# A two-layer transformer trunk on one core: 2048 bytes of descriptor scratch in place of 512, and five small activation buffers in place of six

## The chip, the core and the metric

The kernel runs on one core of a Trainium2 chip. Its engines are TensorE (PE, matrix products), VectorE (DVE), ScalarE (ACT), GpSimd (POOL) and SyncE (SP); each runs its own list of instructions in order, and semaphores hold an instruction back until its inputs are there. Transfers between the off-chip memory (HBM) and the on-chip memory (SBUF, 128 partitions) are issued by SP, ACT or POOL and carried out by 16 DMA engines. The metric is the device time of one execution in microseconds (us). Before the change: median 558.6 of three runs, 558.29 to 560.03.

## What is computed

```python
def reference(x, moba_w_qkv, ..., ln_mlp_b):
    h = x                                     # 1 x 256 x 1024, float32
    for i in range(DEPTH):                    # 2 layers
        if i % 2 == 0:
            mix = moba_attention(h, ...)      # 16 heads of 64
        else:
            mix = dilated_attention(h, ...)   # 12 heads in 3 groups
        h = layer_norm(ALPHA * h + mix, ...)
        h = layer_norm(ALPHA * h + jnp.square(jax.nn.relu(h @ w_in)) @ w_out, ...)
    return h
```

The layers run over 256 tokens of width 1024, and the inner width of the multi-layer perceptron (MLP) is 4096. With 256 tokens and blocks of 256 the block choice of the first layer leaves plain causal attention.

## The kernel before

All weights pass once from HBM through SBUF, and each float32 product is made of three matmuls at reduced input precision: an operand is split into an upper part and a remainder, and upper x upper, upper x lower and lower x upper are added up in PSUM. So each weight tile of 128 x 1024 is loaded by SP into a `raw` buffer (7 of them), ACT writes its upper part to `whi` (L394) and DVE the remainder to `wlo` (L399); `whi` and `wlo` have 10 buffers each. `load_w` (L420) does this. All matmuls stand at L403.

**The second way to load.** `load_far` (L408 to L418) makes the remainder without DVE. ACT copies the upper part (L415) and writes its negative into `wlo` (L416); then POOL issues a transfer from HBM that adds the weight itself onto `wlo` (L417), which leaves weight minus upper part. `FAR` (L41) names the steps that load so: 5 and 14 of the MLP's output projection, in both layers. A step has two tiles, so there are eight such transfers, in four pairs; the tiles meet activations that lie in `sc`. These are the only transfers that POOL issues. The descriptors of a transfer issued by POOL are written into a scratch area of SBUF, whose size, 512 bytes of each partition, is set when the program is made (L1554).

**The MLP.** Its steps are listed in `STEPS`: `f5 f4 f2 f3 O0 f7 f1 O5 f6 ob s2 S8 Oe S4 sa S6 O1 O3 sd O7 o9 z oc Of`. An `f` step multiplies with the first weight matrix, squares and clips. An `o` or `O` step multiplies 256 rows of the second weight matrix. An `s` or `S` step does the same for a two-by-two arrangement of blocks with seven products in place of eight (`do_duo`), from sums of blocks of weights (made by DVE in `raw`) and of activations (`duo_sums`, L637 to L652). `O` and `S` steps have their split activations in the cells of other tensors that are free by then (`sc`, `pt`, `v`, `q0hi` and such); `o` and `s` steps take them from the small activation tiles `ta`.

**The buffers `ta`.** A `ta` tile is 128 x 512 float32, 2048 bytes of each partition. `NTA` (L59) says how many there are. They hold the products of the rotary embedding (L723 and L1102), the squared activations of `O` and `S` steps (`do_first`), the split activations of `o` and `s` steps, and intermediate sums. An `s` step holds five at once: the sums (one) and the two halves each of two splits (four, `spare`, L634). An `o` step holds two. The splits of the step `s2`, the first `s` step, come right behind the step `ob`.

**The order.** The kernel text records operations with a cost each; `Plan.order` (L134 to L304) then simulates the engines and chooses, whenever an engine is free, the operation that can start first (and, of those, the one due first). A buffer is given out when its last user in that simulation is done, so the number of `ta` buffers bears on the order of all engines. The program is then emitted in that order. SBUF is nearly full: the highest address in use ends 256 bytes short of the 229,376 of a partition.

Of the kernel before, what the change touches and what calls it, by code (L numbers as in the profile page):

```python
# [55 lines left out]

OTAGS = {"o": "acc", "p": "tp", "t": "tp"}
HOMES = (("ta", "ta"), ("pt0", "pt1"))
NTA = 6  # L59
NRAW = 7  # L60
NFIRST = 6
PER = 1024 // (NFIRST * P)
# [71 lines left out]
class Plan:  # L134
# [20 lines left out]
    def op(self, eng, cost, fn, reads=(), writes=(), xfer=0.0, early=0.0, ahead=0.0):  # L155
        o = Op()
        o.n, o.eng, o.cost, o.fn, o.xfer = len(self.ops), eng, cost, fn, xfer
        o.early, o.ahead = early, ahead
        o.preds, o.succs, o.bufs = set(), [], set()
        for group, is_write in ((reads, False), (writes, True)):  # L160
            for item in group:
                b, key = item if isinstance(item, tuple) else (item, None)
                o.bufs.add(b)
                for k, st in b.state.items():
                    if key is None or k is None or k == key:
                        if st[0] is not None:
                            o.preds.add(st[0])
                        if is_write:
                            o.preds.update(st[1])
                st = b.state.setdefault(key, [None, []])  # L170
                if is_write:
                    if key is None:
                        b.state = {None: [o, []]}
                    else:
                        st[0], st[1] = o, []
                else:
                    st[1].append(o)
        o.preds.discard(o)
        for p in o.preds:
            p.succs.append(o)  # L180
        for b in o.bufs:
            b.left += 1
            b.ops.append(o)
        self.ops.append(o)
        return o
# [148 lines left out]
def tile_trunk(  # L334
# [37 lines left out]
    def mk(shape, dt, tag, bufs, space=None):  # L372
        uid[0] += 1
        return plan.buf(Bufs(space or sb, bufs), shape, dt, tag, bufs, f"{tag}_{uid[0]}")
# [7 lines left out]
    def act(n, aps=0, sbuf=False):  # L382
        return n / 1200 + (0.093 if sbuf else 0.055) + 0.093 * aps
# [50 lines left out]
    class Stage:  # L434
# [43 lines left out]
        def part(self, j):  # L478
            return next(i for i, (c0, c1) in enumerate(self.parts) if c0 <= S + j * P < c1)
# [154 lines left out]
    def spare():  # L634
        return mk([P, 512], F32R, "ta", NTA), 0, 0

    def duo_sums(u, cells):  # L637

        t, c0, _ = u
        s = mk([P, 512], F32, "ta", NTA)  # L640
        a11, a21, a12, a22 = [part(t, c0 + i * P, P) for i in range(4)]
# [91 lines left out]
    def rotate(xy, ropet):  # L733
# [10 lines left out]
        for half, ps in enumerate(xy):  # L744
            ps = ps()
            b, a = mk([P, 512], F32, "ta", NTA), mk([P, 512], F32, "ta", NTA)
            src = ps
# [122 lines left out]
    def copy_out(n, ps, tag):  # L870
        t = mk([P, 512], F32, tag, NTA if tag == "ta" else 2)
        op("ACT", act(n), lambda: nc.scalar.activation(t.t[:, :n], ps.t[:, :n], AF.Copy), [ps], [t])
        return t
# [238 lines left out]
    def relu_sq_tok(ps, m, ahi, alo):  # L1112
        r = mk([P, 512], F32, "ta", NTA)
        op("ACT", act(512), lambda: nc.scalar.activation(r.t, ps.t, AF.Relu), [ps], [r])
        op("ACT", act(512, 0, True), lambda: nc.scalar.activation(r.t, r.t, AF.Square), [r], [r])
        pt = psum("tp")
        transposes(pt, [(j * P, lambda j=j: r.t[:, j * P : (j + 1) * P]) for j in range(4)], [r], AHEAD["square"])
        t = slice(m * P, (m + 1) * P)
        keys = [(j, m) for j in range(4)]
        split(  # L1120
            512, lambda: pt.t.rearrange("p (j s) -> p j s", j=4), lambda: ahi.t[:, :, t], lambda: alo.t[:, :, t],
            [pt], [(ahi, k) for k in keys], [(alo, k) for k in keys],
        )

    class Mlp:
# [17 lines left out]
        def rest(self, between):  # L1143
# [26 lines left out]
            def do_first(c):  # L1170
                for js in GROUPS:
                    tiles = [(psum("tp"), load_w(win[i][c * 4 + j])) for j in js]
                    mm_wstat_wide(tiles)
                    for k in range(0, len(js), 2):
                        p = 2 * c + js[k] // 2
                        n = {"O": 2, "S": 4}.get(kinds[p], 0)
                        u = cells.take(F32) if not n else (mk([P, 512], F32, "ta", NTA), 0, 0)
                        homes = [cells.take(F32R, True) for _ in range(n)]
# [390 lines left out]
```

## Time and profile before

| | before |
|---|---|
| runs, median (lowest to highest) | 558.6 us (558.29 to 560.03) |
| span of the profiled execution | 557.5 us |
| PE busy | 544.3 us |
| DVE busy | 458.3 us |
| ACT busy | 353.0 us |
| POOL busy | 16.6 us |
| granted PE clock, mean | 0.994 |
| DMA traffic | 109.81 MB, mean 197 GB/s |
| transfers of POOL into `wlo` | 8 of 512 KB, median 8.4 us from issue to landing |

The profile is of one execution, and its span (first to last instruction) stands beside the runs' times, which hold a little more around it; no time of its own besides the span is given for the profiled execution. A row of a timeline has start, duration, engine, line, operation and how many instructions were put together (x2); in brackets stands the time that the engine sat idle before it, and what the profile takes to have ended that. "PEld" are PE's weight loads, which overlap the matmuls. "issue" means that the engine waited for nothing that the profile shows. Names such as `acc<-wlo,sc` say what is written from what.

### The profile page before, as it was taken

What the parts mean: (1) busy time and instruction counts of PE and PEld (TensorE: products, weight loads), DVE (VectorE), ACT (ScalarE), POOL (GpSimd) and SP (SyncE); (2) the same over time, 40 slices, a digit from 0 to 9 for tenths busy, and PEclk for the clock granted to TensorE, in tenths of its full rate; (3) what the DMA queues carried; (4) which work ended last, traced back from release to release, by engine and by line L of the source; (5) the groups of instructions that cost most, each with busy time, mean ns of one, the idle gap of its engine ahead of it and who ended that gap; (6) DMA issues with size and microseconds to landing.
All of it is one profiled execution on the core that took longest, in us unless ns stands there. A gap on an engine that the chain in (4) does not pass through costs nothing.

```text
span 557.5 us, 8613 instructions
## 1 busy us (share of the span) xinstructions
PE 544.3 (98%) x3193; PEld 464.0 (83%) x3193; DVE 458.3 (82%) x785; ACT 353.0 (63%) x566; POOL 16.6 (3%) x23
## 2 busy tenths in 40 slices
PE   9999999999999999899999999999999999979994
PEld 7988888888888888688888889888898888868884
DVE  6798999875786598998989899796787479899847
ACT  6567897336899778566544575625697975856600
POOL 0000000000000000000010000010000100000001
PEclk9999999999999999999999999999999999989998
DMA  8976237267888725877638525308876763766302
GB/s 336 399 301 205 77 114 265 76 202 284 272 280 259 231 81 163 232 222 267 216 140 279 180 75 191 109 4 324 269 272 203 217 223 113 209 169 227 113 2 75
DMA packets 31434, 109.81 MB, mean 197 GB/s; under 512 B 3488, under 2 KB 4384, under 8 KB 31392
## 3 DMA queue, kind: packets, MB, share of 16 engines
q1 hardware_dynamic: 29664, 104.35, 54.6%
q0 software_dynamic: 1152, 4.19, 4.3%
q10 hardware_dynamic: 576, 0.72, 0.4%
q8 instruction: 25, 0.41, 0.3%
q14 instruction: 17, 0.14, 0.1%
HBM read 108.20 MB, written 1.05 MB: 196 GB/s over the span
## 4 chain that ended last, share of the span: by engine, by line
PE 94%; DMA 3%; issue 1%; DVE 1%; ACT 0%; POOL 0%; DVEq 0%; POOLq 0%
PE acc L403 51%; PE tp L403 40%; DMA wlo<-in_wout_dram 3%; PE tp L864 3%; DMA raw<-in_xw_dram 0%; DVE tok L730 0%; POOL rstd L978 0%; ACT whi L394 0%; DVEq L1563 0%; DVE bst L1006 0%; ACT xs L394 0%; DVE bst L1009 0%; DVE mv L976 0%; DVE bst L989 0%; POOLq L1021 0%
## 5 line engine op out<-in xcount | busy, mean ns | idle before, releaser
L394 ACT ACTIVATE whi<-raw 128x1024 fp32r<-128x1024 f32 (+2 forms) x200 | 197.9, 1014 | 87.0 <-PE acc L403 48.9
L399 DVE TENSOR_TENSOR wlo<-raw,whi 128x1024 fp32r<-128x1024 f32 (+2 forms) x202 | 229.2, 1162 | 16.6 <-ACT whi L394 13.8
L403 PE MATMUL tp<-xs,whi 128*128 128x512 f32 x448 | 104.9, 390 | 0.0
L403 PEld LDWEIGHTS tp<-xs,whi 128*128 128x128 f32 x448 | 83.4, 188 | 16.9
L403 PE MATMUL acc<-xs,whi 128*128 128x512 f32 (+1 forms) x272 | 57.2, 357 | 0.1
L403 PEld LDWEIGHTS tp<-xs,wlo 128*128 128x128 f32 x448 | 55.6, 192 | 1.1
L403 PE MATMUL tp<-xs,wlo 128*128 128x256 f32 x448 | 55.9, 283 | 0.0
L403 PEld LDWEIGHTS acc<-xs,whi 128*128 128x128 f32 x272 | 44.6, 190 | 7.7 <-ACT xs L394 0.9
L403 PE MATMUL acc<-whi,ta 128*128 128x512 f32 (+1 forms) x132 | 44.5, 387 | 0.0
L403 PE MATMUL acc<-whi,ahi 128*128 128x512 f32 x104 | 41.1, 395 | 0.0
L403 PE MATMUL acc<-wlo,ahi 128*128 128x512 f32 x96 | 37.4, 390 | 0.0
L403 PE MATMUL acc<-whi,alo 128*128 128x512 f32 x96 | 34.2, 390 | 0.0
L403 PE MATMUL acc<-whi,sc 128*128 128x512 f32 (+1 forms) x98 | 34.0, 397 | 0.0
L403 PE MATMUL acc<-xs,wlo 128*128 128x256 f32 x224 | 30.6, 283 | 0.0
L403 PEld LDWEIGHTS acc<-xs,wlo 128*128 128x128 f32 x224 | 29.2, 191 | 0.9
L403 PE MATMUL acc<-whi,xs 128*128 128x512 f32 (+1 forms) x112 | 28.9, 366 | 0.0
L403 PEld LDWEIGHTS acc<-whi,ta 128*128 128x128 f32 x132 | 24.7, 188 | 4.9
L723 DVE TENSOR_TENSOR ta<-tp,ta 128x256 f32<-128x256 f32 (+1 forms) x36 | 15.9, 450 | 14.5 <-ACT ta L1102 14.4
L403 PE MATMUL acc<-wlo,ta 128*128 128x512 f32 (+1 forms) x66 | 25.5, 386 | 0.0
L403 PE MATMUL tp<-whi,xs 128*128 128x512 f32 x80 | 25.2, 396 | 0.0
L403 PE MATMUL acc<-wlo,sc 128*128 128x512 f32 (+1 forms) x48 | 19.6, 408 | 5.3 <-DMA wlo<-in_wout_dram 5.2
L850 ACT ACTIVATE sc<-sc,mx 128x256 f32<-128x256 f32 (+2 forms) x40 | 19.8, 498 | 6.1 <-DVE mx L840 5.7
(210 smaller groups left out, 854.2 us busy)
## 6 DMA issues: line engine op xcount, KB each, us to landing
raw<-in_win_dram SPq DMA_DIRECT2D x64, 512.0 KB, 4.9
raw<-in_wout_dram SPq DMA_DIRECT2D x64, 512.0 KB, 5.5
raw<-in_wqk_dram SPq DMA_DIRECT2D x22, 512.0 KB, 5.7
raw<-in_wo_dram SPq DMA_DIRECT2D x14, 512.0 KB, 4.3
raw<-in_wv_dram SPq DMA_DIRECT2D x8, 512.0 KB, 5.3
wlo<-in_wout_dram POOLq DMA_DIRECT2D x8, 512.0 KB, 8.4
g<-in_lng_dram SPq DMA_DIRECT2D x4, 512.0 KB, 3.8
b<-in_lnb_dram SPq DMA_DIRECT2D x4, 512.0 KB, 5.1
```

The costliest lines, as they stand in the source:

```text
L394: op("ACT", act(n, sbuf=sbuf), lambda: nc.scalar.activation(hi(), src(), AF.Copy), r, whi)
L399: lambda: nc.vector.tensor_tensor(lo(), src(), f32(hi()), op=ALU.subtract), list(r) + list(whi), wlo,
L403: nc.tensor.matmul(out_ap, lhsT, rhs, start=start, stop=stop)
L723: op("DVE", dve(n) + extra, lambda: nc.vector.tensor_tensor(out_ap(), a(), b(), op=alu), r, w)
L850: lambda: nc.scalar.activation(e(), e(), AF.Exp, bias=bias(), scale=-1.0, accum_out=total()), r, w,
L864: nc.tensor.transpose(ps.t[:, c : c + P], src(), ident.t)
```

## The change

```diff
-NTA = 6
+NTA = 5
...
-    nc = _bacc.Bacc("TRN2", target_bir_lowering=False, num_devices=1, dynamic_dma_scratch_size=512)
+    nc = _bacc.Bacc("TRN2", target_bir_lowering=False, num_devices=1, dynamic_dma_scratch_size=2048)
```

The scratch for descriptors grows by 1536 bytes of each partition, and one `ta` tile less frees 2048. The instructions are the same ones. The orders of SP and POOL stay as they are. Those of ACT and DVE change at some fourteen places per layer, by a few rows each; PE's changes in one place per layer.

That place on PE, in the first layer, is the step `s2`. Names have a running number; `ta_2422` and `ta_2443` are the upper and lower half of the split blocks, `ta_2447` and `ta_2586` (before) or `ta_2592` and `ta_2602` (after) the halves of their sums; `acc` and `tp` are PSUM banks. Of each product of three matmuls only the last one is shown. Before:

```order
L403 MATMUL acc_2090<-whi_2394,ta_2443 128x512
...
L403 MATMUL tp_2592<-whi_2319,ta_2443 128x512
...
L403 MATMUL acc_2093<-whi_2394,ta_2586 128x512
...
L403 MATMUL tp_2609<-whi_2437,ta_2443 128x512
...
L403 MATMUL tp_2616<-whi_2437,ta_2586 128x512
...
L403 MATMUL tp_2623<-whi_2461,ta_2586 128x512
...
L403 MATMUL acc_2104<-whi_2461,ta_2443 128x512
```

And after:

```order
L403 MATMUL acc_2092<-whi_2399,ta_2443 128x512
...
L403 MATMUL tp_2588<-whi_2321,ta_2443 128x512
...
L403 MATMUL tp_2598<-whi_2438,ta_2443 128x512
...
L403 MATMUL acc_2106<-whi_2460,ta_2443 128x512
...
L403 MATMUL acc_2095<-whi_2399,ta_2602 128x512
...
L403 MATMUL tp_2618<-whi_2438,ta_2602 128x512
...
L403 MATMUL tp_2625<-whi_2460,ta_2602 128x512
```

The first product with the sums stands third before and fifth after, behind the four products that need only the blocks themselves. In the second layer it moves by one product, from third to fourth.

On ACT, at the same place in the program, stand the copies of a pair of `load_far` tiles (step 14; L415 and L416). Before, with the split of the sums (`ta_2447`) some ten rows earlier:

```order
L394 ACTIVATE whi_2437<-raw_2162 128x1024
L394 ACTIVATE ta_2447<-ta_2408 128x384
L394 ACTIVATE whi_2461<-raw_2250 128x1024
...
L394 ACTIVATE whi_2554<-raw_2288 128x1024
L415 ACTIVATE whi_2556<-raw_2301 128x1024
L416 ACTIVATE wlo_2568<-whi_2556 128x1024
L415 ACTIVATE whi_2580<-raw_2364 128x1024
L394 ACTIVATE whi_2588<-raw_2398 128x512
L416 ACTIVATE wlo_2598<-whi_2580 128x1024
```

And after:

```order
L394 ACTIVATE whi_2438<-raw_2166 128x1024
L394 ACTIVATE whi_2460<-raw_2252 128x1024
...
L394 ACTIVATE whi_2552<-raw_2292 128x1024
L415 ACTIVATE whi_2554<-raw_2305 128x1024
L416 ACTIVATE wlo_2566<-whi_2554 128x1024
L415 ACTIVATE whi_2578<-raw_2364 128x1024
L394 ACTIVATE whi_2584<-raw_2397 128x512
L394 ACTIVATE ta_2592<-ta_2417 128x384
L416 ACTIVATE wlo_2596<-whi_2578 128x1024
```

The split of the sums, 128 x 384, now stands between the two copies of the second tile, so the L416 on which the second transfer of the pair waits comes one instruction later.

## The prediction

> **What bounds the kernel now.** I read the first and fourth parts of the page, then the list of waits, then the timelines around the only wait that matters.
>
> ```profile
> span 557.5 us, 8613 instructions
> PE 544.3 (98%) x3193; PEld 464.0 (83%) x3193; DVE 458.3 (82%) x785; ACT 353.0 (63%) x566; POOL 16.6 (3%) x23
> PE 94%; DMA 3%; issue 1%; DVE 1%; ACT 0%; POOL 0%; DVEq 0%; POOLq 0%
> ...
> PE acc L403 <- DMA wlo<-in_wout_dram: 5.2, 2, 3.0
> POOL wlo L417 <- issue: 9.8, 1, 9.8
> ```
>
> TensorE (PE) is busy 98% and makes 94% of the chain of work that ended last. The one other entry of weight in the chain, 3%, is a transfer into `wlo` from HBM: the accumulating transfer that POOL issues at L417. PE's matmuls wait for it twice, 5.2 us in all. The change can win only what hangs on these waits.
>
> The timeline of POOL has all eight of these transfers:
>
> ```profile
> 175.51 1.03 POOL L417 DMA_DIRECT2D wlo<-in_wout_dram  x1 [59.91 <-PE acc L403]
> 184.15 0.90 POOL L417 DMA_DIRECT2D wlo<-in_wout_dram  x1 [7.60 <-ACT ta L1102]
> 219.05 0.88 POOL L417 DMA_DIRECT2D wlo<-in_wout_dram  x1 [34.00 <-ACT wlo L416]
> 229.69 0.90 POOL L417 DMA_DIRECT2D wlo<-in_wout_dram  x1 [9.76 <-issue]
> 434.78 0.90 POOL L417 DMA_DIRECT2D wlo<-in_wout_dram  x1 [59.92 <-PE acc L403]
> 443.58 0.89 POOL L417 DMA_DIRECT2D wlo<-in_wout_dram  x1 [7.90 <-ACT ta L1102]
> 478.45 0.87 POOL L417 DMA_DIRECT2D wlo<-in_wout_dram  x1 [33.99 <-PE acc L403]
> 487.81 0.88 POOL L417 DMA_DIRECT2D wlo<-in_wout_dram  x1 [8.49 <-PE tp L403]
> ```
>
> They come in four pairs, and the second of each pair starts 8.6 to 10.6 us after the first. Is its input late? The rows of L416, which makes the `wlo` that the transfer adds to, and the landing of the first of each pair (the view of the tile `wlo` at 175, 219, 434 and 478 us) answer that:
>
> ```profile
> 220.12 1.04 ACT L416 ACTIVATE wlo<-whi 128x1024 fp32r<-128x1024 f32 x1
> ...
> 477.00 1.99 ACT L416 ACTIVATE wlo<-whi 128x1024 fp32r<-128x1024 f32 x2
> ...
> DMA to landing us min/median/max: 8.4/8.4/8.4
> ...
> DMA to landing us min/median/max: 10.3/10.3/10.3
> ...
> DMA to landing us min/median/max: 8.5/8.5/8.5
> ...
> DMA to landing us min/median/max: 9.1/9.1/9.1
> ```
>
> The input is ready at 220.12 + 1.04 = 221.2 and 477.00 + 1.99 = 479.0, yet the instruction starts 8.5 and 8.8 us later. The releasers named in the brackets (ACT, PE tp) had nothing to do with it. What fits is the first transfer's landing: 219.05 + 10.3 = 229.35, and POOL starts at 229.69; 478.45 + 9.1 = 487.55, and POOL starts at 487.81. The other two pairs say the same: 175.51 + 8.4 = 183.9 against 184.15, 434.78 + 8.5 = 443.3 against 443.58. Each second one starts about 0.3 us after the first has landed. So POOL holds the second back until the first has given something back, and the label "issue" (nothing that the profile shows) says that it is no semaphore of the program. Room for descriptors is what the change enlarges.
>
> **What the wait costs.** The rows of PE at the second transfers, and the weight load at the first one of layer 0:
>
> ```profile
> 234.77 0.39 PE L403 MATMUL acc<-whi,sc 128*128 128x512 f32 x1
> 237.38 0.50 PE L403 MATMUL acc<-wlo,sc 128*128 128x512 f32 x1 [2.22 <-DMA wlo<-in_wout_dram]
> ...
> 492.84 0.39 PE L403 MATMUL acc<-whi,sc 128*128 128x512 f32 x1
> 496.21 0.80 PE L403 MATMUL acc<-wlo,sc 128*128 128x512 f32 x1 [2.98 <-DMA wlo<-in_wout_dram]
> ...
> 229.41 0.19 PEld L403 LDWEIGHTS acc<-wlo,sc 128*128 128x128 f32 x1 [0.55 <-DMA wlo<-in_wout_dram]
> ...
> 169.86 5.47 PE acc L403 x24
> ...
> 237.38 6.19 PE acc L403 x26
> ...
> 496.21 5.73 PE acc L403 x17
> ...
> 496.20:502.00 5.80, 5.79 (x19) 4.69 (x19) 5.10 (x9) 2.71 (x4) 0.00 (x0) 0.71 0.50 146
> ```
>
> The rows "x24", "x26" and "x17" are pieces of the chain; the last is a window whose 0.71 is the granted clock. An undisturbed matmul takes 5.47 / 24 = 0.228 us. Layer 0: the matmul after the one at 234.77 would start at 235.00 and starts at 237.38, 2.38 lost; the 26 behind it take 6.19 in place of 26 x 0.228 = 5.93, 0.26 more. Layer 1: due at 493.07, starts at 496.21, 3.14 lost; then the clock falls to 0.71, and 17 matmuls take 5.73 in place of 3.87, 1.86 more. Together **7.64 us**. The short wait at 229.41 (about 0.3 us) belongs to the first transfer of its pair, which nothing moves, so I leave it in.
>
> On the 1.86: the Trainium skill's "TensorE: Matmul & The Clock Gate", section "What's actually happening", has the clock halve after an idle window of about 3.4 us. The idle stretch of 3.14 us here is under that, so by the page's figure the term would be nothing and the saving 5.8 in place of 7.6. The window's 0.71 stands right behind the wait and measurement decides.
>
> **The change, part by part.**
>
> *Four times the scratch (L1554).* If the room is what holds POOL, the second transfer issues when its input is ready, about 221.7 in layer 0 (the new ACT order puts a 0.5 us split ahead of its L416) and 479.3 in layer 1, then stands right behind the first in the same queue. When does it land? The trace of before has no two of them back to back; windows over the packets of queue q0 bound it (the fastest and the slowest of four):
>
> ```profile
> q0 software_dynamic: 144, 0.52, 61.5%
> ...
> q0 software_dynamic: 144, 0.52, 44.2%
> ```
>
> These are 483.0 to 487.3 and 489.5 to 495.9: each holds one whole transfer of 144 packets, which moved in 4.3 and 6.4 us beside the loads that SP issues (6.1 in both of layer 0). One behind the other, the second lands 4.3 to 6.4 us after the first: 233.65 to 235.75 in layer 0, where PE wants it at 235.00, and 491.85 to 493.95 in layer 1, where it is wanted at 493.07. So a wait of 0 to 0.75 and 0 to 0.9 is left. Both middles (234.7 and 492.9) are just in time; I take 0.25 each, **0.5 us**. Waits of this length are shorter than the 2.22 us after which the clock held, so the 1.86 goes too. The first and third pairs cost PE nothing now and nothing after.
>
> What is late next? DVE, which splits the weights, is as good as full behind the stall:
>
> ```profile
> 229.00:243.00 14.00, 11.66 (x51) 9.09 (x50) 13.82 (x21) 8.09 (x10) 0.90 (x1) 1.00 0.66 179
> ...
> 240.17 7.72 DVE L399 TENSOR_TENSOR wlo<-raw,whi 128x1024 fp32r<-128x1024 f32 x7
> ...
> 249.07 0.39 PE L403 MATMUL tp<-wlo,q0lo 128*128 128x512 f32 x1
> ...
> 501.70 2.59 DVE L399 TENSOR_TENSOR wlo<-raw,whi 128x1024 fp32r<-128x1024 f32 x2 [0.70 <-ACT whi L394]
> ...
> 511.52 0.39 PE L403 MATMUL tp<-wlo,q1lo 128*128 128x512 f32 x1
> ```
>
> It doesn't speed up when PE comes earlier. But the tightest `wlo` behind the stall in layer 0 is the first of the seven at 240.17, done 1.2 us later (241.4) and wanted at 249.07: 7.7 us of slack, of which 2.6 go. In layer 1 the first of the two at 501.70 is done at 502.9 and wanted at 511.52: 8.6, of which 5.0 go. At least 3.6 us stay, so the saving is kept. Were that cover gone, it would be paid back in full.
>
> *Five `ta` buffers (L59).* The order of POOL and of SP stays. PE's order differs only in the first two-by-two product group of each layer: the product of `s4` goes back behind two others in layer 0, one in layer 1. Its operands are what one buffer fewer delays, since their tiles must first be released by the step before:
>
> ```profile
> 219.13 0.56 DVE L399 TENSOR_TENSOR ta<-ta,ta 128x384 fp32r<-128x384 f32 x1 [1.22 <-PE acc L403]
> ...
> 219.59 0.63 ACT L394 ACTIVATE whi<-raw 128x512 fp32r<-128x512 f32 x1
> ...
> 205.51 0.50 ACT L394 ACTIVATE ta<-ta 128x384 fp32r<-128x384 f32 x1
> ...
> 222.56 0.61 PE L403 MATMUL tp<-whi,ta 128*128 128x512 f32 x2
> ```
>
> DVE's split waits for such a release already (1.22 us, until 219.13); the next tile is free within a group of three matmuls, 0.7 us, at about 219.8. ACT's half of the split (0.50) moves from 205.51 to behind the row at 219.59 + 0.63, so it ends at about 220.7, and DVE's half (0.56) at about 221.3. In the new order PE reads that last half at 222.56. Slack 1.3 us; the same sum in layer 1 gives about 1. So PE doesn't wait: cost 0, and at worst, were both splits a microsecond later than I reckon, 0.5 us a layer. The gain end is 0 too, as PE waits for no `ta` today. Some sixty rows of ACT and DVE change places by a row or two; with PE's waits all listed above, none of them is on the chain. I put 0 on them, -0.5 to +1 for what I can't see.
>
> **The sum.** 7.64 - 0.5 = 7.1 off the span of 557.5 gives 550.4. The runs' median of 558.6 stands 1.1 above that span; so I predict **551.5 us**.
>
> **Rivals.**
>
> *The room isn't what holds POOL.* All the trace shows is "the second starts when the first has landed", in four pairs of four. A queue that takes one accumulating transfer at a time would look the same, and a larger scratch would do nothing: 558.6. For it: exactness of the 0.3 us. Against: the page's "issue", and that a scratch of 512 is small. Chance 0.07. The Trainium skill speaks for this rival: "DMA: Bandwidth & Descriptors", sections "Terms" and "The descriptor swizzle", has descriptors of 16 bytes and 9 reads and 9 writes per engine and transfer (144 packets over 16 engines agree with the 9). My estimate from that: 512 bytes are 32 descriptors, two transfers 18 in each ring, which would fit already. It fails if a sum takes two reads per row, the weight and what it is added to.
>
> *The eighth transfer still waits.* If 512 bytes hold one transfer and not two, 2048 hold from four to seven, and the ring wraps within the eight. Should the wrap fall on the last and make it wait for its predecessor, layer 1 keeps its 3.14 + 1.86 and only 2.64 - 0.25 go: 556.2. Against it: the oldest room was freed hundreds of microseconds earlier (the transfers at 175 and 184 us). Chance 0.07.
>
> *Slower: the two transfers share.* If the pair's packets alternate in place of queueing, the first lands about as late as the second, some 5 us later, at 234.5. PE wants it at about 229.1 (0.3 before the weight load at 229.41), so it loses 5.4 there, and with a wait over 3 us the clock's 1.9 besides, against 2.9 lost now in this layer: 4.4 worse. In layer 1 the row below has PE at the first one's lower half; it would land at 492.5, a wait of 2.8 and the clock's 1.9, as much as now.
>
> ```profile
> 489.67 0.39 PE L403 MATMUL acc<-wlo,sc 128*128 128x512 f32 x1
> ```
>
> Together 558.6 + 4.4 = 563. It decides from a first landing past about 232. Against: eight packets of an engine in one queue are taken in order, as the compact windows above suggest. Chance 0.04.
>
> **How the numbers follow.** Forecast 0.82: 551.5, by its bounds from 558.6 - 7.64 - 0.3 (the first stall gone too) - 0.5 = 550.2 to 558.6 - 7.64 + 1.65 (both residual waits at their ends) + 1 = 553.6. To leave out no more than 2 in 10 with doubt in my own bounds, the range goes on to the second rival: **550.0 to 556.3**. A measurement tells 0.3% from no change, 1.7 us: faster is below 556.9 (forecast and second rival, 0.89), same the first rival (0.07), slower the third (0.04).
>
> **What would show it.** In the profile after: POOL's second L417 of each pair within 2 us of the first, no "issue" of 8 to 10 us; q0 moving 288 packets in one stretch from 223 to about 235 and from 483 to about 492.5; the waits of PE on `wlo` from HBM under 1 us each; a granted clock of 1.00 behind 490 us; DVE's split of 128x384 at 219 waiting longer on PE, and PE waiting for no `ta`. I am wrong if the second L417 still starts at the first's landing (first or second rival), if the first lands past 232 (third), or if PE shows waits on DVE's `wlo` at 246 or 506 us.

## The result and the profile after

| | before | after |
|---|---|---|
| runs on the same chip, median (lowest to highest) | 559.12 us (558.29 to 560.03, 4 runs) | 552.38 us (551.68 to 553.16, 4 runs) |
| span of the profiled execution | 557.5 us | 550.9 us |
| mean granted PE clock in it | 0.994 | 0.998 |

The ratio on record is 0.9885, 95% interval 0.9859 to 0.9911: faster by 1.15% (the two medians alone would give 0.9879). The line of busy times on the page after, and what is left in the list of waits on the transfers into `wlo` and of POOL's waits before L417:

```profile
PE 542.7 (99%) x3193; PEld 463.5 (84%) x3193; DVE 457.6 (83%) x785; ACT 352.4 (64%) x566; POOL 16.5 (3%) x23
...
PE acc L403 <- DMA wlo<-in_wout_dram: 0.3, 1, 0.3
...
POOL wlo L417 <- PE acc L403: 159.8, 3, 59.8
POOL wlo L417 <- ACT wlo L416: 45.4, 4, 40.3
```

PE's wait of 5.2 us has become 0.3, and POOL no longer waits for "issue". Its timeline shows that the wait before a second transfer now ends with that transfer's own input, ACT's `wlo` of L416 (the last row holds both transfers of its pair):

```profile
175.66 1.03 POOL L417 DMA_DIRECT2D wlo<-in_wout_dram  x1 [59.50 <-PE acc L403]
178.39 0.88 POOL L417 DMA_DIRECT2D wlo<-in_wout_dram  x1 [1.69 <-ACT wlo L416]
219.54 0.88 POOL L417 DMA_DIRECT2D wlo<-in_wout_dram  x1 [40.27 <-ACT wlo L416]
222.43 0.87 POOL L417 DMA_DIRECT2D wlo<-in_wout_dram  x1 [2.01 <-ACT wlo L416]
432.89 0.89 POOL L417 DMA_DIRECT2D wlo<-in_wout_dram  x1 [59.81 <-PE acc L403]
435.23 0.86 POOL L417 DMA_DIRECT2D wlo<-in_wout_dram  x1 [1.44 <-ACT wlo L416]
476.58 1.89 POOL L417 DMA_DIRECT2D wlo<-in_wout_dram  x2 [40.48 <-PE acc L403]
```

The second of a pair starts 1.0 to 2.9 us after the first, not 8.6 to 10.6 as before. When they land (the view of `wlo` on POOL at 219, at 222 and, for both transfers of the last pair, at 477 us), and what queue q0 moves from 223.5 to 232.3:

```profile
DMA to landing us min/median/max: 10.6/10.6/10.6
...
DMA to landing us min/median/max: 10.2/10.2/10.2
...
DMA to landing us min/median/max: 9.8/10.6/11.5
...
q0 software_dynamic: 288, 1.05, 59.9%
```

In layer 0 the first lands at 219.54 + 10.6 = 230.1 and the second at 222.43 + 10.2 = 232.6; in layer 1 at 486.4 and 489.1. Both transfers' packets, 288, go in one stretch. PE at the places where it waited before, and a window behind the one in layer 1:

```profile
230.14 0.50 PE L403 MATMUL acc<-wlo,sc 128*128 128x512 f32 x1 [0.29 <-DMA wlo<-in_wout_dram]
...
235.71 0.39 PE L403 MATMUL acc<-wlo,sc 128*128 128x512 f32 x1
...
491.30 0.39 PE L403 MATMUL acc<-wlo,sc 128*128 128x512 f32 x1
...
488.00:502.00 14.00, 14.00 (x64) 11.58 (x63) 13.82 (x21) 8.53 (x10) 0.00 (x0) 1.00 0.49 166
```

The second transfers are now 3.1 us (235.71 against 232.6) and 2.2 us ahead of their use, there is no wait in brackets, and the granted clock behind the one in layer 1 is 1.00 where it was 0.71. One wait is left, at the first transfer of layer 0's second pair.

Where the time went can be read from the chain of waits, by the starts of two pieces that frame the place in each layer. Before:

```profile
214.08 6.15 PE acc L403 x27
...
251.04 12.92 PE acc L403 x57
...
473.25 6.15 PE acc L403 x27
...
512.13 12.92 PE acc L403 x57
```

And after:

```profile
214.63 4.91 PE acc L403 x22
...
249.25 12.92 PE acc L403 x57
...
471.49 6.15 PE acc L403 x27
...
505.52 12.92 PE acc L403 x57
```

Layer 0: 36.96 became 34.62, 2.34 saved. Layer 1: 38.88 became 34.03, 4.85 saved. Together 7.19. The span gained 6.6, since this execution of the changed kernel was 0.55 us late already at 214 us (214.63 against 214.08).

### The profile page after: what moved, and what is told of

Same layout as the page of the kernel before. It is cut to its first block, busy times and chain, and to the rows that moved or that the text cites. A ratio compares the mean times of both kernels' runs of the same rounds, so it can differ in the third digit from the quotient of the medians.

```text
span 550.9 us, 8611 instructions
## 1 busy us (share of the span) xinstructions
PE 542.7 (99%) x3193; PEld 463.5 (84%) x3193; DVE 457.6 (83%) x785; ACT 352.4 (64%) x566; POOL 16.5 (3%) x23
## 4 chain that ended last, share of the span: by engine, by line
PE 96%; DMA 2%; DVE 1%; POOL 0%; DVEq 0%; ACT 0%; issue 0%; POOLq 0%
PE acc L403 52%; PE tp L403 41%; PE tp L864 3%; DMA wlo<-in_wout_dram 2%; DMA raw<-in_xw_dram 0%; DVE tok L730 0%; POOL rstd L978 0%; DVEq L1563 0%; DVE bst L1006 0%; ACT xs L394 0%; DVE bst L1009 0%; DVE mv L976 0%; DVE bst L989 0%; POOLq L1021 0%; POOLq L978 0%
## 5 line engine op out<-in xcount | busy, mean ns | idle before, releaser
L394 ACT ACTIVATE whi<-raw 128x1024 fp32r<-128x1024 f32 (+2 forms) x200 | 197.1, 1013 | 81.9 <-PE acc L403 40.7
L399 DVE TENSOR_TENSOR wlo<-raw,whi 128x1024 fp32r<-128x1024 f32 (+2 forms) x202 | 228.0, 1160 | 12.6 <-ACT whi L394 10.5
L403 PEld LDWEIGHTS acc<-whi,ahi 128*128 128x128 f32 x104 | 19.5, 188 | 4.1 <-issue 0.3
L403 PEld LDWEIGHTS acc<-whi,xs 128*128 128x128 f32 x112 | 19.8, 188 | 3.7 <-issue 0.3
```

The costliest lines, as they stand in the source:

```text
L394: op("ACT", act(n, sbuf=sbuf), lambda: nc.scalar.activation(hi(), src(), AF.Copy), r, whi)
L399: lambda: nc.vector.tensor_tensor(lo(), src(), f32(hi()), op=ALU.subtract), list(r) + list(whi), wlo,
L403: nc.tensor.matmul(out_ap, lhsT, rhs, start=start, stop=stop)
```

## The experiments

The theory is that POOL holds a transfer back until the scratch has room for its descriptors, that a pair of accumulating transfers doesn't fit into 512 bytes, and that the number of `ta` buffers is worth nothing by itself. The rivals: the new order gains; a queue takes one accumulating transfer at a time; a wrap of the scratch makes a transfer wait.

### The buffers alone: scratch back at 512

```diff
# against the changed kernel
-    nc = _bacc.Bacc("TRN2", ..., dynamic_dma_scratch_size=2048)
+    nc = _bacc.Bacc("TRN2", ..., dynamic_dma_scratch_size=512)
```

> The changed kernel with the scratch put back to 512 bytes; five ta buffers stay, and the order of every engine is that of the changed kernel. Theory (room for descriptors is all that counts): POOL's second L417 of each pair starts 0.2 to 0.4 us after the first has landed, 8 to 11 us after the first's start; PE waits for wlo from HBM about 2.4 us in layer 0 and 3.1 us in layer 1; time 558 to 560, no difference from the kernel before. Rival (the order that five buffers make is what gains): the second starts within 3 us of the first, time 551 to 553. Half and half (the buffers cost or give something by themselves): 556 to 558 or 560.5 and more, with the difference at a PE wait on ta or wlo other than the known two.

Measured: 560.94 us (558.28 to 563.45, 10 runs), against 559.97 (557.81 to 563.66, 17 runs) for the kernel before on that chip; ratio 1.0016, interval 0.9992 to 1.004. The whole gain is gone. The median lies 0.94 above the expected 558 to 560, for a reason that the last two runs of this section show. Rows of POOL's and PE's timelines, one of the chain, and a window of this run:

```profile
219.08 0.88 POOL L417 DMA_DIRECT2D wlo<-in_wout_dram  x1 [32.77 <-ACT wlo L416]
229.60 0.90 POOL L417 DMA_DIRECT2D wlo<-in_wout_dram  x1 [9.63 <-ACT whi L394]
...
237.99 0.79 PE L403 MATMUL acc<-wlo,sc 128*128 128x512 f32 x1 [2.93 <-DMA wlo<-in_wout_dram]
...
237.99 9.11 PE acc L403 x26
...
238.00:244.00 6.00, 6.00 (x14) 4.75 (x15) 4.03 (x7) 1.97 (x2) 0.00 (x0) 0.50 0.44 147
```

The second transfer is back at 10.5 us behind the first, with the order of the changed kernel on every engine, so the order is not what gains. The wait is longer here than in the first profile of before (2.93 against 2.22), and behind it the clock fell to 0.50: the 26 matmuls took 9.11 where they took 6.19.

### The scratch alone: 576 bytes and six buffers

```diff
# against the kernel before
-        mv = mk([P, 2], F32, "mv", 3)
+        mv = mk([P, 2], F32, "mv", 2)
...
-    nc = _bacc.Bacc("TRN2", ..., dynamic_dma_scratch_size=512)
+    nc = _bacc.Bacc("TRN2", ..., dynamic_dma_scratch_size=576)
```

> The kernel before with 64 bytes more scratch (576) and six ta buffers; to make room, the small tile mv has two buffers in place of three, which leaves the order of every engine word for word as it was. Theory (a pair of accumulating transfers needs just over 512 bytes, so 576 holds two): the second L417 starts when its L416 is done, within 3 us of the first, in all four pairs, although the scratch is used round and round with each pair; time 551 to 553, as the changed kernel or up to 0.5 better, since L416 of the second tile isn't behind the split of the sums. Rival (a wrap of the scratch makes a transfer wait): pairs two to four still start at the first's landing, time 556 to 559.5. Rival (more is needed than 576): all four pairs do so, 558 to 560.

Measured: 552.37 us (551.76 to 553.28, 6 runs), ratio 0.9873, interval 0.9851 to 0.9895. The second and third pair on POOL:

```profile
219.33 0.89 POOL L417 DMA_DIRECT2D wlo<-in_wout_dram  x1 [40.34 <-ACT wlo L416]
221.87 0.89 POOL L417 DMA_DIRECT2D wlo<-in_wout_dram  x1 [1.64 <-ACT wlo L416]
433.04 0.91 POOL L417 DMA_DIRECT2D wlo<-in_wout_dram  x1 [59.92 <-PE acc L403]
435.37 0.87 POOL L417 DMA_DIRECT2D wlo<-in_wout_dram  x1 [1.41 <-ACT wlo L416]
```

Sixty-four bytes of each partition do all that 1536 did, with six buffers and the order of before. As the scratch has room for one pair and no more, later pairs must reuse it, and none waits: the rival of the wrap falls, at least for pairs this far apart.

### The changed kernel again, on the same chip

> The changed kernel once more, on the same chip as the run with 576 bytes and six buffers. Theory: 551.5 to 553, the same as that kernel within 0.5 us, since neither the other 1472 bytes nor the sixth buffer is waited for. If the sixth buffer is worth something to PE, this one is slower by 0.5 us or more, with the wait shown at a ta tile. The 0.55 us that the profile of the changed kernel loses before 28 us, where nothing has changed, should be different in this profile if it is a matter of the single execution, and be there again if it comes from the change.

Measured: 552.16 us (552.02 to 553.32, 6 runs), ratio 0.9872, interval 0.985 to 0.9893; the same as with 576 bytes and six buffers. In this profile the chain's first long piece ends at 27.57 us, in the first profile at 28.24: the 0.55 us lost there belonged to that execution, not to the change.

### A plain transfer in place of the sum: 512 and 256 bytes

```diff
# against the kernel before
-  ... nc.gpsimd.dma_start(FAR_OUT(w.lo.t), src, accum_op=ALU.add) ...
+  ... nc.gpsimd.dma_start(FAR_OUT(w.lo.t), src) ...
# and for the second run also
-    nc = _bacc.Bacc("TRN2", ..., dynamic_dma_scratch_size=512)
+    nc = _bacc.Bacc("TRN2", ..., dynamic_dma_scratch_size=256)
```

> The kernel before with L417 as a plain transfer: it writes the weight over wlo in place of adding it (so wlo holds the whole weight and the products are not the reference's); scratch 512 bytes, six buffers, same order. Theory (a sum takes two reads per row, the weight and what it is added to, and so nearly twice the room of a plain transfer): two plain transfers fit into 512 bytes, the second L417 starts when its L416 is done, within 3 us of the first, and PE's waits on wlo are gone or under 0.5 us; about 552. Rival (room goes by bytes or by the number of transfers, or the queue takes one transfer at a time at this size): the second still starts at the first's landing, 8 to 11 us after it, about 558.

> As the run with the plain transfer (L417 writes the weight over wlo, so the products are not the reference's), with the scratch at 256 bytes in place of 512. Theory (room per transfer is what counts: a pair of accumulating ones needs more than 512 and no more than 576 bytes, a plain one about half as much, 9 rows of room against 17, so two plain ones need some 290): at 256 the second L417 starts again at the first's landing, 6 to 9 us after the first's start, though nothing else has changed. Since a plain transfer is faster (it landed within 7 us of its start in the run at 512), PE loses less than before the change: about 0 to 1.5 us per layer, time 551.5 to 555. Rival (only accumulating transfers are held back, whatever the room): the second starts within 3 us, as at 512.

Measured: 551.48 us at 512 bytes and 553.07 at 256, one run each. The second pair on POOL at 512 bytes, then at 256 with the landing of its first:

```profile
218.91 0.54 POOL L417 DMA_DIRECT2D wlo<-in_wout_dram  x1 [40.62 <-ACT wlo L416]
221.50 0.55 POOL L417 DMA_DIRECT2D wlo<-in_wout_dram  x1 [2.05 <-ACT wlo L416]
```

```profile
219.17 0.54 POOL L417 DMA_DIRECT2D wlo<-in_wout_dram  x1 [36.84 <-PE acc L403]
227.95 0.54 POOL L417 DMA_DIRECT2D wlo<-in_wout_dram  x1 [8.23 <-ACT whi L394]
...
DMA to landing us min/median/max: 8.5/8.5/8.5
```

At 512 bytes two plain transfers fit where two accumulating ones don't. At 256 they don't either, and the second starts 0.3 us after the first's landing (219.17 + 8.5 = 227.67), as the accumulating ones did at 512. So it isn't that this queue takes one transfer at a time, and it isn't accumulating transfers alone that are held back: room is what counts, and the sum takes more of it for the same 512 KB. The queue's rows in the pages of the kernel before and of the plain one at 512 bytes say that the moved packets don't show that room:

```profile
q0 software_dynamic: 1152, 4.19, 4.3%
```

```profile
q0 software_dynamic: 1152, 4.19, 2.3%
```

Packets and bytes are equal; only the time of the packets is nearly twice as long with the sum. At 256 bytes PE waited for `wlo` 1.1 us in layer 1 and not at all in layer 0, less than before, since a plain transfer lands sooner (8.5 us after its start where the accumulating one at the same place took 10.3). I had taken the plain transfers at 512 bytes to land within 7 us; the eight of them landed 6.3 to 8.5 us after their starts.

### No transfers from POOL at all

```diff
# against the kernel before
-FAR = (5, 14)
+FAR = ()
```

> FAR is empty: all tiles are split by ACT and DVE, POOL issues no transfer; scratch 512, six buffers; the planner makes a new order of all engines. It asks whether the accumulating transfers pay at all. If DVE's slack behind step 14 (at least 3.6 us after the change, by the prediction) takes the eight extra splits of 1.2 us, two at a time 2.4 us, PE waits for nothing and the time is 551 to 553, as the changed kernel. If DVE has no room for them where they fall, PE waits for wlo from DVE in the step behind and the time is 553 to 558, between the changed kernel and the one before.

Measured: 551.64 us (551.28 to 552.01, 4 runs), ratio 0.9866, interval 0.9829 to 0.9903. DVE makes all remainders, the order of all engines is made anew, no transfer of POOL uses the scratch, and the gain is that of the changed kernel. To set the two against each other they ran on one chip:

> The changed kernel on the same chip as the kernel without POOL's transfers, to compare the two. Theory: both have no wait of weight left on PE, so they are the same within 0.3% (1.7 us); what the changed kernel still pays is the wait of 0.2 to 0.5 us at the first transfer of layer 0's second pair, so it may be up to 0.5 us the slower. Expected 551.5 to 553.

> No POOL transfers (FAR empty), scratch 512, six buffers, on the same chip as the changed kernel. Theory: 551 to 552.5, at most 0.5 us faster than the changed kernel, by the wait at the first transfer that it doesn't have; DVE's eight further splits (about 9 us more busy time) stay hidden behind PE. Rival (the transfers do save PE something elsewhere, where DVE is late without them): slower than the changed kernel by over 0.5 us, with a PE wait on wlo from DVE.

Measured: the changed kernel 552.13 us (551.52 to 552.51, 5 runs), ratio 0.9853, interval 0.9827 to 0.9878; without the transfers 551.26 (551.13 to 551.88, 5 runs), ratio 0.9838, interval 0.9815 to 0.9861. Of the latter, the line of busy times, the only wait in PE's list, and the pieces of the chain that frame the two places:

```profile
PE 541.9 (99%) x3193; PEld 462.8 (84%) x3193; DVE 465.9 (85%) x793; ACT 345.9 (63%) x558; POOL 9.4 (2%) x15
...
PE tp L403 <- PEq L1554: 0.8, 1, 0.8
...
213.97 6.15 PE acc L403 x27
...
248.00 12.92 PE acc L403 x57
...
470.22 6.15 PE acc L403 x27
...
504.25 12.92 PE acc L403 x57
```

With no wait in them, the two stretches take 34.03 us each. (So they do with plain transfers at 512 bytes, in the order of before: 214.00 to 248.03 and 470.26 to 504.29.) So the stalls had cost 36.96 - 34.03 = 2.93 us in layer 0 of the first profile, the first transfer's part included, and 38.88 - 34.03 = 4.85 in layer 1; of that 0.59 and nothing are left in the profile after the change.

PE waits for no weight at all, with DVE 8.3 us busier than in the changed kernel's first profile (465.9 against 457.6). The difference of 0.9 us between the medians is more than the 0.5 expected, but the intervals overlap and so do the runs; that it is faster than the changed kernel stays open. The rival, that the transfers save PE something, falls: against this order without them they did not pay, and with 512 bytes they cost over 1%.

### The kernel before, twice more, for its clock

> The kernel before once more, for its clock. The theory says that the spread of its runs (557.8 to 563.7 in 17 of them, where the changed kernel has 551.7 to 553.3) comes from the two waits of 2 to 3.4 us: in some executions the clock falls behind one, in some behind both. Then this profile shows about 2.4 and 3.1 us of waiting again, and the span is 557.5 if the clock falls behind one of them, 559.5 if behind both, 555.5 if behind none. Rival: the spread comes from elsewhere, such as the first 28 us or the transfers; then the span differs from 557.5 with the clock as in the first profile.

> The same kernel a second time, for a second sample: the span follows the number of waits behind which the clock falls (about 1.9 us each), as in the run ahead of it.

The times were 562.31 and 560.77 us, one run each. PE's wait in layer 0, and three windows of 3.41 us around it (the busy time of PE is the first number behind the length, the granted clock the third from the end), first for the one, then for the other:

```profile
237.05 0.65 PE L403 MATMUL acc<-wlo,sc 128*128 128x512 f32 x1 [1.95 <-DMA wlo<-in_wout_dram]
...
233.83:237.25 3.42, 1.48 (x7) 0.94 (x6) 3.33 (x5) 2.06 (x3) 0.00 (x0) 1.00 0.74 184
237.25:240.66 3.41, 3.41 (x9) 2.66 (x9) 3.41 (x7) 1.62 (x2) 0.00 (x0) 0.50 0.59 191
240.66:244.07 3.41, 3.41 (x17) 2.81 (x16) 2.20 (x3) 2.30 (x3) 0.00 (x0) 1.00 0.41 123
```

```profile
236.75 0.50 PE L403 MATMUL acc<-wlo,sc 128*128 128x512 f32 x1 [1.95 <-DMA wlo<-in_wout_dram]
...
232.51:235.93 3.42, 2.29 (x11) 1.56 (x9) 3.37 (x5) 2.53 (x3) 0.00 (x0) 1.00 0.90 188
235.93:239.34 3.41, 2.59 (x11) 2.18 (x12) 3.38 (x6) 0.56 (x1) 0.00 (x0) 1.00 0.89 286
239.34:242.75 3.41, 3.41 (x16) 2.81 (x15) 3.35 (x6) 3.41 (x5) 0.00 (x0) 1.00 0.11 32
```

The same wait of 1.95 us, and the clock falls behind it in one execution and not in the other. What differs is where the wait lies. In all twelve profiles of this case the granted clock (the share of full speed that PE is given) is either 1.00 or 0.50, and within an execution its changes are whole multiples of 3.413 us apart. (The two falls of the first execution here, at 237.25 and 496.66, are 76 such steps apart.) Where the steps lie differs from execution to execution. The windows above are such steps; for the second execution they are counted back from its fall in layer 1, at 495.34. In the first execution the wait of 1.95 lies within one step and leaves PE 1.48 us of work there; in the second it is cut in two and leaves 2.29 and 2.59.

The same holds for every step at full clock in the twelve profiles: where PE was busy at most 1.48 us, the next step ran at half clock, and where it was busy 1.74 us or more, the next kept full clock. The wait of 2.22 us in the first profile, behind which the clock held, was cut into 1.65 and 0.57. A step at half clock, if PE works all through it, costs half its length, 1.71 us. Of the six falls behind these waits, where PE still waited within the slow step, the next step was slow too (three), and where it didn't, the clock came back (three).

All four profiles with the long waits, with the sum of the four columns and its distance from the first:

| profile | wait, layer 0 | 26 matmuls behind | wait, layer 1 | 17 matmuls behind | sum | span |
|---|---|---|---|---|---|---|
| before | 2.22 | 6.19 | 2.98 | 5.73 | 17.12 | 557.5 |
| before, second | 1.95 | 7.78 | 3.90 | 6.50 | 20.13 (+3.01) | 560.5 (+3.0) |
| before, third | 1.95 | 6.19 | 3.97 | 6.74 | 18.85 (+1.73) | 559.0 (+1.5) |
| scratch 512, five buffers | 2.93 | 9.11 | 3.24 | 5.75 | 21.03 (+3.91) | 561.4 (+3.9) |

The spans follow the sums within 0.3 us. So the spread of the kernel before (557.81 to 563.66 in 17 runs, against 552.02 to 553.32 for the changed one) is, in the profiles at hand, the length of the two waits and what the clock does behind them; and five buffers with 512 bytes show no cost of their own (the runs' interval, up to 1.004, would leave room for 2.2 us; the profile, for 0.3). My expected spans for these two runs were 557.5, 559.5 or 555.5 and missed, because I had put the waits as fixed and the clock's share at 1.9 each time; behind one wait the clock was slow for no step, one or two.

## Why the prediction was right

Forecast 551.5 us in a range of 550.0 to 556.3; measured 552.38. Step by step:

- **The room for descriptors holds POOL.** Right, and shown by the scratch alone (576 bytes) and by the buffers alone. The first rival of the prediction, another cause for the wait, is out.
- **The descriptor estimate from the Trainium skill spoke against it.** "DMA: Bandwidth & Descriptors", sections "Terms" and "The descriptor swizzle", gave, by my estimate, 18 descriptors of 16 bytes for two transfers, 288 bytes, which should fit into 512. (The page counts them for one transfer of 1 MiB to 128 partitions; these are of 512 KB, to 128 partitions as well.) The runs bound it: a plain pair needs more than 256 bytes and at most 512, which agrees with the 288; an accumulating pair needs more than 512 and at most 576. By 16 bytes each, an estimate, that is over 16 and at most 18 descriptors for one accumulating transfer, so the reading "a sum takes two reads per row", 17, fits, and the 9 can hold for plain ones only. That it is reads was not shown, only the room.
- **2.64 less 0.25 in layer 0, 5.00 less 0.25 in layer 1.** Measured 2.34 and 4.85 from the chain, 7.19 in all against 7.14. That they meet so well is in part luck, since two errors of 0.3 us cancel. First, both losses were put about 0.15 too high: the 6.19 and 5.73 run from the start of their first matmul, the 0.228 are taken from pieces that run from end to end, and a matmul's record lasts 0.39, so 0.16 of each is no loss but the length of that first record. In layer 1 that leaves 3.14 + 1.71 = 4.85, what the frame of 34.03 gives and what was saved. Second, the residual isn't where I put it: the second transfers are not late at all. They land 2.5 and 2.7 us after the first ones, where my bounds, from single transfers, said 4.3 to 6.4. What remains in layer 0 is the wait at the first transfer, which grew from 0.3 to 0.45 us (230.14 against 229.46 + 0.23); in the three further profiles of kernels whose accumulating pairs are not held back, the wait in brackets there was 0 to 0.6. A second transfer can come later than these two: with 576 bytes the one in layer 1 landed 3.8 us behind its first, and the stretch there took 34.35 us (471.52 to 505.87), 0.3 more than without a wait.
- **The clock.** The term of 1.86 was read from one execution; in that one it was 1.71, one step at half clock. The step "waits shorter than the 2.22 us after which the clock held" was wrong as a rule: it fell behind 1.95 us in one execution, since the place of a wait in the steps counts with its length. It did no harm as no such wait was left.
- **From the span to the time.** Here a term was mis-sized. The forecast put the time 1.1 us above the span, from a median and a span that need not belong together. In every execution with both on record, the time is about 1.8 above the span (552.71 and 550.9, 562.31 and 560.5). With 1.8 the sum's 550.4 would have given 552.2, where 552.38 was measured; this is most of the 0.9 by which the forecast was low.
- **The start from 558.6.** That median of three runs was low: 559.12 with the fourth run, 559.63 to 560.06 in the longer series, and the profiled execution (557.5) had the clock fall behind only one wait. Against the series with the changed kernel on the same chip (559.97 and 560.06) the gain is 7.8 and 7.9 us, more than the 7.1 forecast; the waits and the clock together cost the average execution more than they cost that one.
- **Cover behind the stall.** Right: DVE is busy 13.82 of 14 us in the window quoted from either profile (layer 0 before, layer 1 after), and PE waits for no `wlo` of its making.
- **Five buffers cost nothing.** Right, by the run with 512 bytes. DVE's half of the sums' split, and the last matmul of PE's first product with the sums, after:

```profile
221.41 0.55 DVE L399 TENSOR_TENSOR ta<-ta,ta 128x384 fp32r<-128x384 f32 x1
...
223.11 0.39 PE L403 MATMUL acc<-whi,ta 128*128 128x512 f32 x1
```

The split is done at 221.96 and read at 223.11, a slack of 1.15 us where I had reckoned 1.3. That DVE would wait longer for PE there was wrong: the split's row shows no wait, and DVE's idle time of 2.33 us stands one instruction earlier and is put down to ACT (`whi`, L394).

- **The other rivals.** The eighth transfer didn't wait. If the two transfers shared the engines, it did the first little harm: it lands 10.6 us after its start, before 10.3. Of the signs, the second start within 2 us was too narrow: three of the four pairs took 2.3 to 2.9.

## What to carry to other kernels

When an engine that issues transfers starts one just after the landing of the one before, in every pair, and no semaphore of the program explains it, look at the room for descriptors, and give it what the largest number of transfers in flight needs: accumulating transfers took more room than plain ones, and 64 bytes more were enough here. A wait of 2 to 4 us on TensorE can cost up to about twice its length through the clock (2.93 us of waiting and 3.0 behind it in the run with 512 bytes and five buffers), differently in each execution, so a single profile may understate what its removal is worth. And before mending a path, ask whether it is needed: without these transfers the kernel was at least as fast.

## What the runs showed that I had not expected

- The clock fell behind waits of PE of 1.95 (once of twice), 2.93, 2.98, 3.24, 3.90 and 3.97 us, not behind 2.22. What tells them apart in the twelve profiles is PE's work within one step of 3.41 us: at most 1.48 us of it and the next step was slow, 1.74 or more and it was not. The Trainium skill, "TensorE: Matmul & The Clock Gate", section "What's actually happening", has the clock fall after an idle window of about 3.4 us and calls the window free-running. The traces agree with its length (3.413 us) and with the free run; they differ in that the window need not be idle, as the clock fell after one with 1.48 us of work.
- A plain transfer of 512 KB occupied POOL for 0.53 to 0.58 us, an accumulating one for 0.86 to 0.91 (the first of a run 0.71 to 0.72 and 1.03 to 1.04), though they move the same packets.
- Two accumulating transfers in one queue landed 2.5 to 3.8 us apart in the four profiles where they were not held back, though single ones had taken 4.3 to 6.4 us to move.
